# A decoder layer with a gathered and a dense expert mixer on one core: the gather's steps and pace rewritten, four expert blocks' gates kept in SBUF

## The chip, the cores and the metric

One core of a Trainium2 chip runs the whole layer as one program. The metric is the device time of one execution in microseconds; lower is better. The core has a matrix engine (PE), a vector engine (DVE), an activation engine (ACT), a general engine (POOL) and a queue engine (SP), each with its own instruction queue worked off in order, and 16 DMA engines that all of them share.

## The reference

One inference step: attention and mLSTM heads, cross attention, and then the part that matters here, a PEER mixer over 16,384 experts. Each token has 8 heads that choose 16 experts each, so 128 experts with a gate `g`:

```python
e = jnp.take_along_axis(cidx, j, axis=-1)          # 8 x 16 expert numbers per token
g = jax.nn.softmax(sc, axis=-1)
a = g * jax.nn.gelu(jnp.einsum('td,thkd->thk', xb, peer_u[e]))
y = jnp.einsum('thk,thkd->td', a, peer_v[e])
```

`peer_u` and `peer_v` are 16,384 rows of 1,024 float32 each (67 MB each). There are 512 prompt tokens in tiles 0 to 3 of 128, and 32 sample tokens (tile 4).

## The kernel before

Tile 0 goes through all sub-layers first (group 0), then tiles 1 to 3 and the sample tokens together (group 1). The mixer is computed in two ways side by side.

**Gathered tokens** (tiles 0, 3 and 4; class `Gather`). 32 tokens by their 128 experts are one part. For its 32 steps an indirect DMA on POOL's queue gathers 128 rows of one table into a [128, 1024] tile (512 KB): `ru` rows of `peer_u`, of which DVE takes the dot product with the token rows `xr` (`u_load`; three `ru` buffers), or `rv` rows of `peer_v` (`v_load`; six buffers), which PE multiplies, two tiles to a group, by a small matrix `Z` that DVE fills with the gated activations (`v_group`: 4 products, 8 PE instructions, `y<-rv,Z`). Tile 0's u side is done while group 1 runs (`hidden`). What is left for `Gather.steps`, a generator in which each `yield` follows one load, are 4 parts of tile 0 (v side only, 128 loads) and 5 parts of tiles 4 and 3 (u and v, 160 loads each): 448 loads. The old generator has two loops: 4 x 32 v loads of tile 0; then, once the part's choice is known (`G.known`), part after part the u loads of one with the v loads of the part before. Its first part there (tile 4) has no part before it, so 32 u loads stand alone, and the last 32 v loads too.

**Dense tokens** (tiles 1 and 2, 256 tokens; class `Dense`). All 128 blocks of 128 experts are computed. `u_block`: 8 float32 products (16 PE instructions, `ph<-xw,ut`) for the first 40 blocks, and for the other 88, issued from inside the loop below, 24 float32r products (`ph<-xT2..`) of a tile `ut` split into two parts by ACT and DVE; then Gelu into `h`. `gates` builds for each token the 128 x 128 matrix of its gates: DVE and ACT write one-hot tiles `O1` and `O2`, PE multiplies them into `pgt`, ACT copies that to `stg`, and SP writes `stg` to a DRAM tensor `Gd`, one DMA for each of 8 groups of 32 tokens. `v_block`: SP loads `Gt` (gates of four blocks, from `Gd`) and `vt` (two blocks of `peer_v`), DVE makes `a = h * Gt`, `a` and `vt` are split, and PE does 12 float32r products of 512 columns into `yd` (`v_products`).

**What orders them.** A compiler pass schedules instructions by program order as priority. The program order is made by two pacers. `te` adds up a nominal time for each PE product emitted (0.42e-3 a column for float32r, 1.7e-3 for float32; products inside a step are not counted) and runs one step of `Gather.steps` for every `te.every` units. `v` does the same with DVE work and runs one of the first 40 `u_block`s per step. `te.every` is `EVERY3` from the choices (`choices[i].rest()`, DVE's top-16 work) on, and `EVERY4` from block `dn.FIRST` = 13 of the v loop on. With `G.strict` a dot product on DVE also waits for the PE product last emitted.

The end of the program in order: choices (DVE top-16, with early u blocks and gathers), gates (with the last of 40 u blocks), 128 v blocks with u blocks 40 to 127 running 27 ahead, and a layer norm of the two dense tiles. The last two blocks are done one dense tile after the other.

Of the kernel before, what the change touches and what calls it, by code (L numbers as in the profile page):

```python
# [10 lines left out]
F32 = mybir.dt.float32  # L11
F32R = mybir.dt.float32r
# [8 lines left out]
D = 1024  # L21
# [172 lines left out]
def program(ctx, tc, I, O, dbg=None):  # L194
    nc = tc.nc
    dbg = dbg or {}
    s, g = nc.scalar, nc.gpsimd
# [52 lines left out]
    v, te = Vector(nc.vector), Tensor(nc.tensor)  # L250
# [9 lines left out]
    DR = ctx.enter_context(tc.tile_pool(name="scratch", bufs=1, space=bass.MemoryType.DRAM))  # L260
# [51 lines left out]
    right = {}  # L312
# [13 lines left out]
    def split(hi, lo, src):  # L326

        s.copy(hi, src)  # L328
        v.behind(v.tensor_sub(lo, src, hi))

    def parts(raw, hi, lo):
        split(hi, lo, raw)
        return hi, lo
# [103 lines left out]
    TD = 128 * len(DT)  # L437
# [1 line left out]
    memVd = DR.tile([128, 2 * D], F32, name="memVd")  # L439
    x0d = DR.tile([544, D], F32, name="x0d")  # L440
    x2d = [DR.tile([128 if i < 4 else NS, D], F32, name=f"x2d{i}") for i in range(5)]
    Gd = DR.tile([TD // 32, 128, 128, 32], F32, name="Gd")
    eT = {i: P1.tile([128, 128 if i < 4 else NS], I32, name=f"eT{i}") for i in range(5) if i not in DT}
    iT = {}
    gT = {i: P1.tile([128, 128 if i < 4 else NS], F32, name=f"gT{i}") for i in range(5)}
# [1050 lines left out]
    class Gather:  # L1496
# [95 lines left out]
        def steps(self):  # L1592


            us, vs, prev = [], [], None

            parts = [(0, 32 * o) for o in range(4)]
            for o, (i, c) in enumerate(parts):
                p = {"o": o, "parts": parts, "e": eT[i][:, c:c + 32], "hT": gT[i][:, c:c + 32]}
                for k in range(32):  # L1600
                    if k % 2 == 0:
                        rows = []
                    self.v_load(p, k, rows)
                    if k % 2:
                        vs.append((self.late, p, k // 2, rows))
                    vs = [(n - 1, *w) for n, *w in vs]
                    if vs and vs[0][0] < 0:
                        self.v_group(*vs.pop(0)[1:])
                    yield
            parts = []  # L1610
            for r in self.rounds:
                parts += [(r, o) for o in range(len(r))]
            ahead = None
            for n, part in enumerate(parts + [None]):
                p, ahead = ahead, None
                if part and not p:
                    r, o = part
                    while r[o][0] not in self.known:
                        yield
                    p = self.begin(r, o)  # L1620
                for k in range(32):
                    if k == 24 and n + 1 < len(parts) and parts[n + 1][0][0][0] in self.known:
                        ahead = self.begin(*parts[n + 1])
                    if p:
                        us.append(self.u_load(p, k))
                        if prev and self.strict:
                            yield
                    if prev:
                        if k % 2 == 0:
                            rows = []  # L1630
                        self.v_load(prev, k, rows)
                        if k % 2:
                            vs.append((self.late, prev, k // 2, rows))
                    if us and (len(us) == self.ub or not p):
                        us.pop(0)()
                    vs = [(n - 1, *w) for n, *w in vs]
                    if vs and vs[0][0] < 0:
                        self.v_group(*vs.pop(0)[1:])
                    yield
                prev = p  # L1640
            for w in vs:
                self.v_group(*w[1:])

# [36 lines left out]

    def gates(X, PX):

        copy = None
        for tg in range(TD // 32):
            stg = X.tile([128, 128, 32], F32, name="stg", tag="stg", bufs=2)
            i, t0 = DT[tg // 4], 32 * (tg % 4)
            for q in range(8):
                t4 = t0 + 4 * q
                O1 = X.tile([128, 4, 128], F32, name="O1", tag="O1", bufs=4)
                v.tensor_tensor(O1, cst["iota"][:, None, :].to_broadcast([128, 4, 128]), iT[i][:, 0, t4:t4 + 4, None].to_broadcast([128, 4, 128]), op=OP.is_equal)  # L1690
                p = PX.tile([128, 512], F32, name="pgt", tag="pgt", bufs=4)
                for k in range(4):
                    O2 = X.tile([128, 128], F32, name="O2", tag="O2", bufs=12)
                    t = slice(t4 + k, t4 + k + 1)
                    if k:
                        v.tensor_scalar(O2, cst["iota"], iT[i][:, 1, t], gT[i][:, t], op0=OP.is_equal, op1=OP.mult)
                    else:

                        s.activation(O2, cst["iota"], AF.Square, bias=iT[i][:, 2, t])
                        s.activation(O2, O2, AF.Relu, bias=gT[i][:, t], scale=iT[i][:, 3, t])  # L1700
                    te.matmul(p[:, 128 * k:128 * k + 128], O2, O1[:, k], start=True, stop=True)
                if copy:
                    copy()

                def copy(tg=tg, q=q, stg=stg, p=p):
                    s.copy(stg[:, :, 4 * q:4 * q + 4], p.rearrange("p (k j) -> p j k", k=4))
                    if q == 7:
                        nc.sync.dma_start(Gd[tg], stg)
        copy()

    class Dense:
# [3 lines left out]
        def __init__(self, X, XF, PH_, xT):  # L1715
# [7 lines left out]
            for o in (0, 4):  # L1723
                t = right["weights"].tile([128, 4, TD], F32, name="xw", tag="wh", bufs=2)
                v.tensor_add(t, self.xhi[:, o:o + 4], self.xlo[:, o:o + 4])
                self.xw += [t[:, k] for k in range(4)]

        def rows(self, X, c):
            if c % 2 == 0:
                self.two = X.tile([128, 2, D], F32, name="vt", tag="vt", bufs=2)  # L1730
                nc.sync.dma_start(self.two.rearrange("p a d -> p (a d)"), I["peer_v"][128 * c:128 * c + 256].rearrange("(p a) d -> p (a d)", a=2))
            return parts(self.two[:, c % 2], *(X.tile([128, D], F32R, name="vt" + x, tag="vt" + x, bufs=2) for x in "hl"))
# [22 lines left out]

        def v_block(self, X, c):
            n = TD // 32
            if c % 4 == 0:
                self.G = X.tile([128, n, 128], F32, name="Gt", tag="Gt", bufs=2)
                nc.sync.dma_start(self.G.rearrange("p g (a t) -> p g a t", a=4), Gd[:, :, c:c + 4].rearrange("g p a t -> p g a t"))  # L1760
            G = self.G[:, :, 32 * (c % 4):32 * (c % 4) + 32]
            vh_, vl = self.rows(X, c)
            a = X.tile([128, TD], F32, name="a", tag="a", bufs=2)
            by = lambda t: t.rearrange("p (g t) -> p g t", t=32)
            v.tensor_tensor(by(a), by(self.h.pop(c)), G, op=OP.mult)
            ah, al = (X.tile([128, TD], F32R, name=x, tag=x, bufs=3) for x in ("ah", "al"))
            split(ah, al, a)
            return c, ah, al, vh_, vl
# [74 lines left out]
    with tc.tile_pool(name="group0", bufs=1) as Gp:  # L1843
        with weights("weights0", 4):
            xT0 = transposed(0, Gp, xt0)
            rows = sample_index(SL)
# [13 lines left out]
    LATER = 200  # L1860
    EVERY = 2.6
    EVERY2 = 2.6
    EVERY3 = 1.0
    EVERY4 = 1.85
    SKIP = 4
    NZ = 2
    W1 = weights("weights1", 2)
# [33 lines left out]
    dn = Dense(XU, XF, PU, xT2)  # L1901
    EU1 = 3.5
    EU2 = 5.8
# [7 lines left out]
    G.strict = True  # L1911
    te.start(G.steps(), EVERY3)
    for i in (4,) + DT + (3,):
# [2 lines left out]
        G.known.add(i)  # L1916
    stackC.close()
    stackN.close()
    v.every = EU2

    with tc.tile_pool(name="psum gates", bufs=1, space=PSUM) as PX:
        gates(stackC.enter_context(tc.tile_pool(name="gates", bufs=1, side="right")), PX)
    v.finish()
    stackC.close()
    with tc.tile_pool(name="dense v", bufs=1, side="right") as X, tc.tile_pool(name="psum dense", bufs=1, space=PSUM) as PD:
        y = PD.tile([128, len(DT), 1024], F32, name="yd")
        for b in range(NK - 2):
            if b == dn.FIRST:
                stackF.close()
                dn.XT = stackT.enter_context(tc.tile_pool(name="dense ut", bufs=1))  # L1930
                te.every = EVERY4
            if b >= dn.FIRST and b + dn.LA < NK:
                dn.u_block(b + dn.LA)
            w = dn.v_block(X, b)
            for j in range(len(DT)):
                dn.v_products(y, j, *w)

        te.finish()
        last = [dn.v_block(X, b) for b in range(NK - 2, NK)]
        for j in range(len(DT)):  # L1940
            for q in range(2):
                for w in last:
                    dn.v_products(y, j, *w, qs=(q,))
            dn.end(X, y, j)
    stackT.close()
    stackU.close()
    stackG.close()
    stackX.close()

# [13 lines left out]
```

## Time and profile before

| | us |
|---|---|
| median of three runs | 2233.27 (2228.27 to 2234.23) |
| the profiled execution, its own time | 2213.07 |
| its span, first to last instruction | 2211.3 |
| PE busy / DVE / ACT / POOL | 1891.7 / 1427.5 / 677.2 / 833.2 |
| bytes moved by DMA | 625.89 MB, mean 283 GB/s |

A busy PE is a union of pipelined instructions whose ends are modelled, so 99% busy is not 99% of peak. The profile lists each product of float32 as two PE instructions. Times of the trace are from the span's start.

### The profile page before, as it was taken

What the parts mean: (1) busy time and instruction counts of PE and PEld (TensorE: products, weight loads), DVE (VectorE), ACT (ScalarE), POOL (GpSimd) and SP (SyncE); (2) the same over time, 40 slices, a digit from 0 to 9 for tenths busy, and PEclk for the clock granted to TensorE, in tenths of its full rate; (3) what the DMA queues carried; (4) which work ended last, traced back from release to release, by engine and by line L of the source; (5) the groups of instructions that cost most, each with busy time, mean ns of one, the idle gap of its engine ahead of it and who ended that gap; (6) DMA issues with size and microseconds to landing.
All of it is one profiled execution on the core that took longest, in us unless ns stands there. A gap on an engine that the chain in (4) does not pass through costs nothing. (4 is left out here: it accounts for less than half of the span.)

```text
span 2211.3 us, 31987 instructions
## 1 busy us (share of the span) xinstructions
PE 1891.7 (86%) x11579; PEld 1453.3 (66%) x11579; DVE 1427.5 (65%) x3650; ACT 677.2 (31%) x1285; POOL 833.2 (38%) x715
## 2 busy tenths in 40 slices
PE   6998989879787697789899864678998899999997
PEld 4876757759756574567555553446786787786786
DVE  5234334769688784277996476757676777775666
ACT  2121222222333222123112322423343344343443
POOL 3010331026544341130455453445565655563200
PEclk9988999989889897889999985878999999999999
DMA  9626686459957777655799997999999999999854
GB/s 311 215 83 161 177 268 218 164 150 342 286 171 250 261 275 284 232 186 131 272 374 376 351 335 256 340 366 344 386 403 348 377 403 404 402 405 354 305 189 165
DMA packets 213711, 625.89 MB, mean 283 GB/s; under 512 B 23298, under 2 KB 88898, under 8 KB 198578
## 3 DMA queue, kind: packets, MB, share of 16 engines
q0 software_dynamic: 94272, 327.45, 41.3%
q1 hardware_dynamic: 107872, 281.00, 36.1%
q10 hardware_dynamic: 11410, 15.41, 2.0%
q8 instruction: 92, 1.51, 0.3%
q14 instruction: 65, 0.53, 0.1%
HBM read 593.10 MB, written 30.66 MB: 282 GB/s over the span
## 5 line engine op out<-in xcount | busy, mean ns | idle before, releaser
L241 DVE SCALAR_TENSOR_TENSOR ru<-ru,xr 128x1024 f32<-128x1024 f32 x288 | 348.7, 1218 | 200.6 <-DMA ru<-in_peer_u,idx 167.1
L1516 POOL DMA_INDIRECT rv<-in_peer_v,eT x288 | 339.5, 1179 | 311.2 <-PE y L245 240.5
L1516 POOL DMA_INDIRECT ru<-in_peer_u,idx x160 | 211.9, 1325 | 319.4 <-DVE ru L241 162.9
L1673 POOL DMA_INDIRECT ru<-in_peer_u,idx x128 | 166.7, 1302 | 165.2 <-DVE ru L241 106.2
L245 PE MATMUL y<-rv,Z 128*32 128x512 f32 x1152 | 173.8, 651 | 61.6 <-DMA rv<-in_peer_v,eT 41.2
L245 PE MATMUL ph<-xT2h,utl 128*128 128x256 f32 x704 | 202.2, 287 | 15.4 <-DVE utl L241 15.3
L245 PE MATMUL ph<-xT2h,uth 128*128 128x256 f32 x704 | 200.7, 285 | 7.7 <-ACT uth L328 7.5
L245 PE MATMUL ph<-xT2l,uth 128*128 128x256 f32 x704 | 202.8, 288 | 0.0
L245 PE MATMUL yd<-vth,ah 128*128 128x512 f32 x512 | 164.0, 399 | 8.8 <-ACT ah L328 6.8
L245 PE MATMUL yd<-vtl,ah 128*128 128x512 f32 x512 | 163.3, 398 | 7.1 <-DVE vtl L241 7.1
L245 PE MATMUL yd<-vth,al 128*128 128x512 f32 x512 | 163.3, 398 | 0.0
L241 DVE TENSOR_TENSOR vtl<-vt,vth 128x1024 fp32r<-128x1024 f32 x128 | 156.3, 1222 | 10.7 <-ACT vth L328 6.1
L328 ACT CAST vth<-vt 128x1024 fp32r<-128x1024 f32 x128 | 134.4, 1051 | 69.6 <-DMA vt<-in_peer_v 31.9
L245 PE MATMUL ph<-xw,ut 128*128 128x256 f32 x640 | 155.4, 390 | 0.0
L245 PEld LDWEIGHTS ph<-xT2h,utl 128*128 128x128 f32 x704 | 134.6, 191 | 26.9 <-DVE utl L241 16.6
L245 PEld LDWEIGHTS ph<-xw,ut 128*128 128x128 f32 x640 | 118.1, 193 | 50.7 <-issue 31.9
L328 ACT CAST uth<-ut 128x1024 fp32r<-128x1024 f32 x88 | 92.6, 1052 | 187.8 <-PE ph L245 146.8
L245 PEld LDWEIGHTS ph<-xT2h,uth 128*128 128x128 f32 x704 | 136.2, 193 | 20.2 <-issue 8.4
L245 PEld LDWEIGHTS ph<-xT2l,uth 128*128 128x128 f32 x704 | 135.6, 193 | 14.8 <-issue 11.4
L245 PE MATMUL pgt<-O,O 128*128 128x128 f32 x512 | 94.1, 331 | 53.7 <-DVE O L241 51.4
L245 PEld LDWEIGHTS pgt<-O,O 128*128 128x128 f32 x512 | 79.1, 225 | 83.4 <-DVE O L241 56.9
L245 PEld LDWEIGHTS yd<-vtl,ah 128*128 128x128 f32 x512 | 96.5, 190 | 39.4 <-DVE vtl L241 10.5
(541 smaller groups left out, 3717.6 us busy)
## 6 DMA issues: line engine op xcount, KB each, us to landing
vt<-in_peer_v SPq DMA_DIRECT2D x64, 1024.0 KB, 9.4
ut<-in_peer_ut SPq DMA_DIRECT2D x44, 1024.0 KB, 12.3
ut<-in_peer_ut SPq DMA_DIRECT2D x40, 512.0 KB, 6.7
Gd<-stg SPq DMA_DIRECT2D x8, 2048.0 KB, 11.0
Gt<-Gd SPq DMA_DIRECT2D x32, 512.0 KB, 11.8
wz<-in_w_z SPq DMA_DIRECT2D x30, 512.0 KB, 4.8
wo<-in_w_out SPq DMA_DIRECT2D x16, 512.0 KB, 11.1
wz<-in_w_mq SPq DMA_DIRECT2D x16, 512.0 KB, 5.9
```

Of the source, the lines that this page charges most:

```text
L241: return lambda out, *a, **k: self.count(f(out, *a, **k), 0.06 + math.prod(out.shape[1:]) / 960)
L245: return self.count(self.e.matmul(out, l, r, **kw), math.prod(r.shape[1:]) * (0.42e-3 if r.dtype == F32R else 1.7e-3))
L328: s.copy(hi, src)
L1516: self.last = g.indirect_dma_start(out=t, out_offset=None, in_=I[table], in_offset=bass.IndirectOffsetOnAxis(ap=idx, axis=0))
L1673: g.indirect_dma_start(out=t, out_offset=None, in_=I["peer_u"], in_offset=bass.IndirectOffsetOnAxis(ap=idx[:, k:k + 1], axis=0))
```

## The change

`steps` becomes one loop: `ready` holds parts whose v side can run, first the four of tile 0; in each round of 32 steps the v loads of the oldest ready part run beside the u loads of the next part, if that one was begun. The next part is begun at step 24 when its choice is known and at most one part is ready. `EVERY3` goes from 1.0 to 1.25, a new `EVERY5` = 1.65 holds in the gates, and `EVERY4` = 1.75 (was 1.85) holds from block 0 of the v loop on. The gates of blocks 0 to 3 are copied by ACT straight from `pgt` into an SBUF tile `Gt`, which lives in a pool of its own opened ahead of the gates; `Gd` and `stg` hold the other 124. The `peer_v` rows of blocks 0 to 3 are loaded into the weight buffers of the u blocks ahead of the last `Gd` write (`early`). `O2` has 9 buffers for 12.

```diff
--- before.py
+++ after.py
-    Gd = DR.tile([TD // 32, 128, 128, 32], F32, name="Gd")
+    Gd = DR.tile([TD // 32, 128, 124, 32], F32, name="Gd")
...
-            us, vs, prev = [], [], None
+            us, vs, ahead, n = [], [], None, 0
 
             parts = [(0, 32 * o) for o in range(4)]
-            for o, (i, c) in enumerate(parts):
-                p = {"o": o, "parts": parts, "e": eT[i][:, c:c + 32], "hT": gT[i][:, c:c + 32]}
+            ready = [{"o": o, "parts": parts, "e": eT[i][:, c:c + 32], "hT": gT[i][:, c:c + 32]} for o, (i, c) in enumerate(parts)]
+            parts = [(r, o) for r in self.rounds for o in range(len(r))]
+            known = lambda: n < len(parts) and parts[n][0][parts[n][1]][0] in self.known
+            while ready or n < len(parts):
+                p, ahead = ahead, None
+                prev = ready.pop(0) if ready else None
+                if not p and not ready and n < len(parts):
+                    while not known() and not prev:
+                        yield
+                    if known():
+                        p = self.begin(*parts[n])
+                n += p is not None
                 for k in range(32):
-                    if k % 2 == 0:
-                        rows = []
-                    self.v_load(p, k, rows)
-                    if k % 2:
-                        vs.append((self.late, p, k // 2, rows))
-                    vs = [(n - 1, *w) for n, *w in vs]
-                    if vs and vs[0][0] < 0:
-                        self.v_group(*vs.pop(0)[1:])
-                    yield
-            parts = []
-            for r in self.rounds:
-                parts += [(r, o) for o in range(len(r))]
-            ahead = None
-            for n, part in enumerate(parts + [None]):
-                p, ahead = ahead, None
-                if part and not p:
-                    r, o = part
-                    while r[o][0] not in self.known:
-                        yield
-                    p = self.begin(r, o)
-                for k in range(32):
-                    if k == 24 and n + 1 < len(parts) and parts[n + 1][0][0][0] in self.known:
-                        ahead = self.begin(*parts[n + 1])
+                    if k == 24 and known() and len(ready) + (p is not None) <= 1:
+                        ahead = self.begin(*parts[n])
                     if p:
                         us.append(self.u_load(p, k))
                         if prev and self.strict:
...
-                prev = p
+                if p:
+                    ready.append(p)
...
+        G0 = dn.gates_tile()
         for tg in range(TD // 32):
-            stg = X.tile([128, 128, 32], F32, name="stg", tag="stg", bufs=2)
+            stg = X.tile([128, 124, 32], F32, name="stg", tag="stg", bufs=2)
...
-                    O2 = X.tile([128, 128], F32, name="O2", tag="O2", bufs=12)
+                    O2 = X.tile([128, 128], F32, name="O2", tag="O2", bufs=9)
...
-                    s.copy(stg[:, :, 4 * q:4 * q + 4], p.rearrange("p (k j) -> p j k", k=4))
+                    pj = p.rearrange("p (k j) -> p j k", k=4)
+                    s.copy(stg[:, :, 4 * q:4 * q + 4], pj[:, 4:])
+                    s.copy(G0[:, tg].rearrange("p (a t) -> p a t", a=4)[:, :, 4 * q:4 * q + 4], pj[:, :4])
                     if q == 7:
+                        if tg == TD // 32 - 1:
+                            dn.early()
                         nc.sync.dma_start(Gd[tg], stg)
...
+        def gates_tile(self):
+            self.G = self.XW.tile([128, TD // 32, 128], F32, name="Gt", tag="Gt", bufs=2)
+            return self.G
+
+        def early(self):
+
+            self.rows0 = []
+            for c in range(4):
+                t = right["weights"].tile([128, D], F32, name="vt0", tag=("w", "wl")[c % 2], bufs=2)
+                nc.sync.dma_start(t, I["peer_v"][256 * (c // 2):256 * (c // 2) + 256].rearrange("(p a) d -> p a d", a=2)[:, c % 2])
+                self.rows0.append(t)
+
         def rows(self, X, c):
+            if c < 4:
+                return parts(self.rows0[c], *(X.tile([128, D], F32R, name="vt" + x, tag="vt" + x, bufs=2) for x in "hl"))
...
-            if c % 4 == 0:
-                self.G = X.tile([128, n, 128], F32, name="Gt", tag="Gt", bufs=2)
-                nc.sync.dma_start(self.G.rearrange("p g (a t) -> p g a t", a=4), Gd[:, :, c:c + 4].rearrange("g p a t -> p g a t"))
+            if c and c % 4 == 0:
+                nc.sync.dma_start(self.gates_tile().rearrange("p g (a t) -> p g a t", a=4), Gd[:, :, c - 4:c].rearrange("g p a t -> p g a t"))
...
-    EVERY3 = 1.0
-    EVERY4 = 1.85
+    EVERY3 = 1.25
+    EVERY4 = 1.75
+    EVERY5 = 1.65
...
-    v.every = EU2
-
+    v.every, te.every = EU2, EVERY5
+
+    stackW = ExitStack()
+    dn.XW = stackW.enter_context(tc.tile_pool(name="block gates", bufs=1, side="right"))
...
+        te.every = EVERY4
         for b in range(NK - 2):
             if b == dn.FIRST:
                 stackF.close()
                 dn.XT = stackT.enter_context(tc.tile_pool(name="dense ut", bufs=1))
-                te.every = EVERY4
```

## Rows read from the trace of the kernel before

**Rows 1.** The page: the span, and the busy tenths of PE, DVE and DMA and the GB/s in 40 slices of 55.3 us.

```profile
span 2211.3 us, 31987 instructions
...
PE   6998989879787697789899864678998899999997
...
DVE  5234334769688784277996476757676777775666
...
DMA  9626686459957777655799997999999999999854
GB/s 311 215 83 161 177 268 218 164 150 342 286 171 250 261 275 284 232 186 131 272 374 376 351 335 256 340 366 344 386 403 348 377 403 404 402 405 354 305 189 165
```

**Rows 2.** Busy time by stretch, all instructions: choices, gates in three parts, the change-over, blocks 0 to 12, blocks 13 to 92, u and v without gathers, v alone, layer norm. Columns: stretch, its length, busy us of PE, PEld, DVE, ACT and POOL with counts, granted clock, DMA share, GB/s.

```profile
core 0: us, PE busy (x) PEld busy (x) DVE busy (x) ACT busy (x) POOL busy (x), PEclk, DMA share, GB/s
1058.00:1197.00 139.00, 128.62 (x663) 76.02 (x661) 111.47 (x564) 22.83 (x48) 72.82 (x71) 0.98 0.93 348
1197.00:1262.00 65.00, 56.08 (x364) 37.43 (x361) 38.18 (x113) 29.53 (x68) 31.82 (x32) 0.95 0.95 357
1262.00:1366.00 104.00, 63.00 (x299) 49.26 (x302) 73.00 (x154) 28.67 (x65) 51.17 (x46) 0.75 0.86 302
1366.00:1424.00 58.00, 41.78 (x242) 29.57 (x238) 44.79 (x122) 30.57 (x67) 25.23 (x23) 0.84 0.87 319
1424.00:1454.00 30.00, 10.83 (x51) 1.69 (x52) 6.00 (x15) 3.72 (x6) 12.13 (x13) 0.59 1.01 381
1454.00:1520.00 66.00, 49.61 (x194) 33.83 (x194) 44.73 (x73) 19.74 (x26) 29.18 (x23) 0.86 0.98 361
1520.00:2068.00 548.00, 522.92 (x3317) 416.12 (x3317) 378.68 (x609) 216.65 (x319) 303.42 (x224) 0.97 1.00 382
2068.00:2120.00 52.00, 52.00 (x340) 45.14 (x339) 34.15 (x48) 23.55 (x35) 1.95 (x2) 1.00 0.62 220
2120.00:2196.00 76.00, 74.80 (x333) 61.42 (x331) 52.73 (x75) 37.99 (x52) 0.00 (x0) 1.00 0.61 208
2196.00:2211.00 15.00, 3.30 (x14) 2.17 (x12) 10.89 (x20) 0.00 (x0) 1.98 (x2) 0.77 0.19 70
```

**Rows 3.** The gates, 1197 to 1424 us: groups of instructions by line. Columns: count, busy us, mean ns of one, idle time before them and what ended it.

```profile
L245 PE MATMUL pgt<-O,O 128*128 128x128 f32 x512 | 94.1, 331 | 53.7 <-DVE O L241 51.4 <-ACT O L1700 1.2 <-DVE Z L241 0.2
...
L241 DVE TENSOR_SCALAR O<-cst,iT,gT 128x128 f32<-128x128 f32 x189 | 57.9, 351 | 8.2 <-PE pgt L245 7.9
L241 DVE SCALAR_TENSOR_TENSOR ru<-ru,xr 128x1024 f32<-128x1024 f32 x46 | 56.1, 1222 | 39.9 <-DMA ru<-in_peer_u,idx 35.7 <-PE pgt L245 3.2 <-PE ph L245 0.6
L1516 POOL DMA_INDIRECT ru<-in_peer_u,idx x46 | 53.3, 1158 | 61.5 <-DVE O L241 37.8 <-DVE ru L241 17.4 <-DVE hT L241 2.4
L1516 POOL DMA_INDIRECT rv<-in_peer_v,eT x50 | 53.3, 1065 | 52.2 <-PE y L245 43.4 <-PE pgt L245 4.3 <-issue 4.0
...
L241 DVE TENSOR_TENSOR O<-cst,iT 128x512 f32<-128x512 f32 x62 | 42.3, 682 | 0.0
L1706 ACT COPY stg<-pgt 128x512 f32<-128x512 f32 x63 | 36.7, 582 | 91.7 <-PE pgt L245 91.5
```

**Rows 4.** DMA in the same stretch, 1197 to 1424 us: all packets, and POOL's queue of gathers (q0).

```profile
DMA packets 17659, 73.13 MB, mean 322 GB/s; under 512 B 2396, under 2 KB 2396, under 8 KB 16748
...
q0 software_dynamic: 14380, 50.93, 64.0%
```

**Rows 5.** The timeline from the last copy of the gates on, with the first `yd` products of blocks 0 (1453.69), 4 (1467.59), 13 (1517.89) and 101 (2123.58), found by counting 12 `yd` products a block. Columns: start, duration, engine, line, what, and idle time before it.

```profile
1424.02 0.58 ACT L1706 COPY stg<-pgt 128x512 f32<-128x512 f32 x1 [1.92 <-PE pgt L245]
...
1424.63 0.32 SPq L1708 DMA_DIRECT2D Gd<-stg  x1
...
1434.46 0.37 SPq L1760 DMA_DIRECT2D Gt<-Gd  x1
1434.89 2.27 SPq L1731 DMA_DIRECT2D vt<-in_peer_v  x2
...
1444.19 0.76 DVE L241 TENSOR_TENSOR a<-h,Gt 128x256 f32<-128x256 f32 x2 [2.23 <-DMA Gt<-Gd]
...
1447.78 1.99 ACT L328 CAST vth<-vt 128x1024 fp32r<-128x1024 f32 x2 [1.16 <-DMA vt<-in_peer_v]
...
1453.69 1.22 PE L245 MATMUL yd<-vth,ah 128*128 128x512 f32 x2
...
1467.59 0.62 PE L245 MATMUL yd<-vth,ah 128*128 128x512 f32 x2
...
1517.89 1.22 PE L245 MATMUL yd<-vth,ah 128*128 128x512 f32 x2 [0.42 <-ACT ah L328]
...
2123.58 0.61 PE L245 MATMUL yd<-vth,ah 128*128 128x512 f32 x2
```

**Rows 6.** Unit costs, each the busy time of one tile's instructions in one stretch (PE first): `yd` with v blocks alone, `ph` where u and v blocks run without gathers, `y` in blocks 13 to 92.

```profile
2120.00:2190.00 70.00, 69.14 (x306) 57.39 (x307) 0.00 (x0) 1.00 0.62 211
...
2077.00:2120.00 43.00, 23.10 (x185) 23.10 (x186) 2.63 (x7) 1.00 0.53 187
...
1520.00:2068.00 548.00, 68.06 (x488) 9.74 (x488) 8.89 (x13) 0.97 1.00 382
```

**Rows 7.** DMA from 1520 to 2068 us, blocks 13 to 92: all packets, and the GB/s in 40 slices of that stretch.

```profile
GB/s 297 338 352 382 398 410 400 407 404 403 407 395 294 295 277 414 396 412 398 413 397 411 399 409 400 409 396 408 402 407 400 407 404 400 409 343 347 322 400 330
DMA packets 64923, 209.53 MB, mean 382 GB/s; under 512 B 5931, under 2 KB 26635, under 8 KB 54671
```

**Rows 8.** The same stretch, groups by line: DVE's dot products of gathered rows.

```profile
L241 DVE SCALAR_TENSOR_TENSOR ru<-ru,xr 128x1024 f32<-128x1024 f32 x97 | 118.4, 1221 | 124.2 <-DMA ru<-in_peer_u,idx 102.4 <-PE yd L245 10.3 <-PE ph L245 9.1
```

More of the change, by code (lines that the diff above doesn't have):

```diff
@@ L1635, in steps @@
                         us.pop(0)()
-                    vs = [(n - 1, *w) for n, *w in vs]
+                    vs = [(w[0] - 1, *w[1:]) for w in vs]
                     if vs and vs[0][0] < 0:
@@ L1946, in program @@
     stackU.close()
+    stackW.close()
     stackG.close()
```

## The prediction, made before the kernel was run

> **What bounds it now.** Read the 40 slices first [rows 1]: from about 1060 us on DMA stands at 9 tenths nearly throughout, and only the last three slices fall back, to 305, 189 and 165 GB/s. The dip of PE to 6 tenths is in the middle of that. So the gathers use DMA early, and the last 130 us use half of it. The stretches [rows 2] say what each stage is held by. In the choices PE (128.6 of 139 us) and DVE (111.5) are both nearly full. The gates take 227 us, with DVE busy 38.2 + 73.0 + 44.8 = 156 us, PE 161 us and DMA moving 322 GB/s on the mean: nothing is full. The middle part is the worst, 104 us at a granted clock of 0.75: the products wait 51.4 us for `O` on DVE, and DVE itself waits 35.7 us for gathered `ru` rows [rows 3]. That is the stretch where u loads stand alone on three buffers, each dot product blocking DVE's queue, and with it the next `O`. Then come 29.7 us from the last copy at 1424.0 to the first `yd` at 1453.7 [rows 5]: `Gd` must land before `Gt` is issued (1434.5), `vt` stands behind `Gt` on SP, and its cast starts at 1447.8. Blocks 0 to 12 run at 361 GB/s with PE at 50 of 66 us. Blocks 13 to 92 are the long stretch: 548 us, DMA share 1.00 at 382 GB/s and PE busy 522.9. There both are at their limit. After 2068 no gather is left; PE is full and DMA at 0.6.
>
> **The pace in loads.** From the code's nominal units. A float32 u block is 8 x 256 x 1.7e-3 = 3.48 units. Choices: 28 u blocks and some transposes, 99 units, 99 loads before and 99 / 1.25 = 79 after. Gates: 256 products of 128 columns (55.7) and 12 u blocks (41.8), 97.5 units: 97 loads before, and the trace has 46 + 50 = 96 [rows 3], so the count holds; after, 97.5 / 1.65 = 59. Blocks 0 to 12: 12 x 512 x 0.42e-3 = 2.58 units each, 33 loads before, 33.5 / 1.75 = 19 after. From block 13 on u and v are 5.16 units together: 2.79 loads a block before, which uses up the last 220 by block 92; after, 2.95 a block, 260 by block 100, and 31 remain at 1.47 a block, to block 122. A load is 50.93 MB / 96 = 0.53 MB [rows 4]. So 58 loads (31 MB) leave choices and gates, 14 leave blocks 0 to 12, and 71 go behind block 13, 31 of them into the stretch that DMA now half uses.
>
> **Unit costs.** 69.14 / 306 = 0.226 us for a `yd` product, so 2.71 us a v block; 23.10 / 185 = 0.125 for `ph`, 3.0 us a u block; 68.06 / 488 x 8 = 1.12 us for a gather group, which is two v loads [rows 6]. By tile sizes a u and v block moves 0.52 + 0.52 + 0.13 = 1.18 MB, a v block alone 0.66.
>
> **Choices.** 20 loads fewer are 10 groups, at most 11 us of PE. DVE's top-16 work stays. Between 0 and -11: I take -4, since DVE is almost as full as PE.
>
> **Gates.** Three bounds. By bytes: 73.1 MB [rows 4] less 37 loads (19.6), less one layer norm that moves behind (1.5), plus the early `peer_v` rows (2.1): 54 MB, which is 141 us at the 382 GB/s of blocks 13 to 92 and 168 us at this stretch's own 322. By DVE: 64 `O` of 0.682 and 192 of 57.9 / 189 = 0.306 are 102 us, 21 dots of 1.30 are 27, the rest 7: 136 us, and at the old busy share (156 / 227) 198 us. So 141 to 198. In detail: the first 30%, v loads alone, was 65 us at 357 GB/s and PE 56; with 0.6 of the loads, 55 to 60. The rest had 162 us for 98 us of DVE work as it will be; its last part, u and v mixed, kept DVE busy 44.8 / 58 = 77%, so 98 to 127. That makes 153 to 187; I take 171, so -56. What the change adds here is covered: 64 more small ACT copies (below the 0.58 us of the `stg` copy, so under 37 us) on an ACT that was busy 89 of 227; `O2` with 9 buffers still holds two rounds of four.
>
> **Change-over and blocks 0 to 12.** Blocks 0 to 3 need neither `Gd` nor `vt` any more. Block 4 does: `Gt` and `vt` wait on SP behind the last `Gd` write as before, so its cast comes 24 us after the last copy and its first product about 27, where now it comes at 1467.6, 43.6 after [rows 5]. The gain is thus 17 us, not the 30 that the gap shows: what is late next is `Gt` of block 4. If the new tiles must wait until `stg` has been written out (10 us, 1424.6 to 1434.5), blocks 0 to 3 still fit ahead of block 4. Blocks 4 to 12 took 50 us, to 1517.9; now 9 x (0.66 + 1.47 x 0.53) = 13 MB at 382 is 34 us. Sum 62 us for 94, -32, between -16 (no gain in blocks 4 to 12) and -40.
>
> **Blocks 13 to 100.** Before 2123.6 - 1517.9 = 606 us [rows 5]. After: 1.18 + 2.95 x 0.53 = 2.74 MB a block, PE 5.71 + 0.74 x 1.12 = 6.54 us. At 382 GB/s 7.17 us, at the 400 to 410 of the flat part of [rows 7] 6.8. I take 7.05, nearer the mean, since PE is not the limit then: 620 us, +15. Ends: 6.8, -6, and 7.6 at the 361 GB/s of blocks 0 to 12, +62.
>
> **Blocks 101 to 127.** 27 blocks took 76 us [rows 2]; plus 15.5 groups of 1.12: 93; by bytes 22 x 1.44 / 382 = 83 + 14 = 97. I take 96, +20 (17 to 25). The last layer norm of gathered rows falls here, beside a DVE that is busy 52.7 of 76 us.
>
> **Sum.** -4 - 56 - 32 + 15 + 20 = -57. The profiled execution took 2213.07 for a span of 2211.3; 2156 after. The runs' median is 2233.27 / 2213.07 = 1.0091 of it: 2176 us.
>
> **A rule against it.** Blocks 13 to 92 moved 382 GB/s for 548 us, and slices of 400 to 410 follow one another [rows 7]. The Trainium skill, page "DMA: Bandwidth & Descriptors", section "Bandwidth", has about 358 GB/s as what the memory gives one core, and says that this side binds transfers between memory and SBUF. The trace does not agree, by 7% on the mean. An estimate by that page: 2.74 / 358 = 7.65 us a block, 673 us for 88, and the sum would be about nothing.
>
> **Rivals.**
> 1. Gates little shorter: DVE's in-order queue keeps its old busy share, 198 us. For it: `O` waits behind dots whatever the pace. Against it: the u loads no longer stand alone. Then -30: 2203.
> 2. DMA full at its best: gates 141, blocks 13 to 100 at 400 GB/s (602 us, -4), change-over -37, choices -4, the end +17. That is -114: 2118. For it: 200 us at 400 GB/s and more [rows 1]; against it: PE at 6.54 us leaves 4% for every wait.
> 3. The moved bytes pay in full: with more gathers for each block, DMA falls to the 361 GB/s of blocks 0 to 12, which had 33 gathers beside 13 blocks of 0.66 MB [rows 2]. Blocks 13 to 100 +62, the end +25, the change-over -31, the gates and choices as forecast: -4, 2229, no change. This is also where the page's rule ends. Against it: [rows 7].
> 4. Slower: late dots. 97 dots waited 102.4 us for `ru`, 1.05 each [rows 8], with three buffers, and a load is now asked for 5% sooner while DMA is full. DVE does 378.7 / 78 = 4.86 us a block; with 1.48 dots a block for 1.24 it is 5.16, 454 us for 88, plus 130 dots. At 1.05 each that is 591, under 620; at 2.1 it is 727, +122, the sum +50: 2284. It decides from 1.7 us a dot, 7.7 us a block.
>
> **Chances and range.** Forecast 0.55, rival 1 0.20, rival 2 0.13, rival 3 0.07, rival 4 0.05. The forecast's own range, gates 153 to 187 and blocks 13 to 100 within 20 us, is 2145 to 2207. The range reaches down to rival 2 and up over rival 1 to just short of rival 3: 2118 to 2220. A change under 0.3% (6.7 us) cannot be told here. Faster 0.88 (forecast, rivals 1 and 2), same 0.06 (most of rival 3), slower 0.06 (rival 4 and a rest).
>
> **What would show it.** 59 loads between the first `pgt` and the last `stg` copy, and 153 to 187 us there, with no stretch at a clock of 0.75; the first `yd` under 15 us after the last copy and block 4 near 27, held by `Gt` or `vt`; `rv` loads until a few us before the last `yd`; 370 GB/s and more from block 101 on. Wrong if DVE's idle time for `ru` in the blocks passes 1.7 us a dot, if the gates stay above 200 us, or if DMA at share 1.00 shows under 370 GB/s.

## The result and the profile after

The changed kernel took 2154.0 us (median of six runs, 2148.6 to 2159.1) against 2230.8 us (2217.6 to 2238.6) for the kernel before, run beside it: a ratio of 0.964, interval 0.961 to 0.967. That is 77 us less; the forecast was 57. One execution of 4866 us, of the last experiment's second kernel, is left out of all that follows. The first lines of the page after, by 40 slices of 53.8 us:

```profile
span 2152.9 us, 32053 instructions
...
PE   6998989878888778688999998879979979999997
...
DVE  5234324497778786437899687767666757777666
...
DMA  9635675728965859756489999999999999999996
GB/s 320 217 88 138 187 242 184 243 82 269 320 227 177 305 161 355 242 207 218 114 280 350 355 383 390 385 338 399 405 329 371 405 342 369 405 405 405 398 370 228
```

Against [rows 1], PE's dip in slices 24 to 27 has gone from 6, 4, 6 and 7 tenths to 9, 8, 8 and 7, and DMA's last slices stand at 405, 398, 370 and 228 where they stood at 354, 305, 189 and 165. The stages of the changed kernel, in the columns of [rows 2]: choices, gates, blocks 0 to 12 with the change-over, blocks 13 to 100, blocks 101 to 127, layer norm.

```profile
1056.00:1200.00 144.00, 133.79 (x679) 88.89 (x676) 131.08 (x701) 30.18 (x63) 57.45 (x56) 0.99 0.81 292
1200.00:1339.00 139.00, 133.06 (x855) 97.50 (x853) 112.33 (x304) 89.56 (x261) 57.54 (x58) 1.00 0.98 379
1339.00:1399.00 60.00, 48.13 (x218) 33.12 (x219) 42.20 (x75) 23.46 (x35) 22.25 (x19) 0.94 1.01 377
1399.00:2035.00 636.00, 585.36 (x3669) 463.45 (x3667) 444.12 (x717) 239.50 (x354) 356.02 (x268) 0.96 1.01 381
2035.00:2142.00 107.00, 98.40 (x464) 62.12 (x460) 69.88 (x122) 36.14 (x51) 37.63 (x33) 0.98 0.89 329
2142.00:2153.00 11.00, 0.25 (x2) 0.00 (x0) 6.86 (x13) 0.00 (x0) 0.99 (x1) 0.69 0.26 95
```

The same two stages of the kernel before, cut at the same marks (the choices from the last `pm` product ahead of them, and blocks 13 to 100):

```profile
1038.00:1197.00 159.00, 146.63 (x745) 90.80 (x744) 131.23 (x706) 29.98 (x63) 72.82 (x71) 0.98 0.86 318
1518.00:2124.00 606.00, 580.92 (x3680) 466.36 (x3681) 415.48 (x661) 242.00 (x357) 305.64 (x227) 0.97 0.97 367
```

Stage by stage, in us, with the gathered loads issued there:

| stage | before | after | change | forecast | loads before, after |
|---|---|---|---|---|---|
| choices | 158.9 | 143.8 | -15 | -4 | 71, 55 |
| gates | 227.5 | 139.7 | -88 | -56 | 96, 58 |
| last copy to block 13 | 93.3 | 60.1 | -33 | -32 | 35, 19 |
| blocks 13 to 100 | 605.7 | 635.8 | +30 | +15 | 218, 258 |
| blocks 101 to 127 | 76.7 | 106.7 | +30 | +20 | 0, 30 |
| sum | | | -76 | -57 | |

**The two spans must not be subtracted.** 2211.3 - 2152.9 is 58, which looks like the forecast to the microsecond. But the choices, the first place that the change touches, begin at 1038 in one profile and at 1056 in the other, after identical work; in a second profile of the changed kernel (below) they begin at 1040 and its span is 2133.6. Counted from the choices on, the change is -76, as the medians have it.

The gates' groups after, in the columns of [rows 3]:

```profile
L245 PE MATMUL pgt<-O,O 128*128 128x128 f32 x511 | 69.3, 282 | 4.3 <-ACT O L1692 2.2 <-DVE O L241 1.4 <-issue 0.6
...
L241 DVE SCALAR_TENSOR_TENSOR ru<-ru,xr 128x1024 f32<-128x1024 f32 x19 | 23.2, 1224 | 10.4 <-PE pgt L245 4.2 <-DMA ru<-in_peer_u,idx 3.9 <-PE ph L245 2.2
```

Before, PE stood 53.7 us ahead of `pgt`, 51.4 of them for `O`; now 4.3. DVE waited 35.7 us for gathered rows, now 3.9. At a granted clock of 1.00 (before, 0.75 in the middle part [rows 2]) a `pgt` product takes 282 ns for 331, which over 512 products is 25 us of PE time. PE is busy 133 of 139 us.

### The profile page after: what moved, and what is told of

Its sections match the earlier page's. It is cut to its first block, busy times and chain, and to the rows that moved or that the text cites. A ratio compares the mean times of both kernels' runs of the same rounds, so it can differ in the third digit from the quotient of the medians.

```text
span 2152.9 us, 32053 instructions
## 1 busy us (share of the span) xinstructions
PE 1878.7 (87%) x11579; PEld 1437.4 (67%) x11579; DVE 1421.5 (66%) x3650; ACT 676.2 (31%) x1349; POOL 836.5 (39%) x715
## 5 line engine op out<-in xcount | busy, mean ns | idle before, releaser
L245 PEld LDWEIGHTS yd<-vth,al 128*128 128x128 f32 x512 | 96.4, 190 | 35.0 <-issue 15.1
L1086 POOL DMA_INDIRECT kvb<-in_pool_lat,ixk x64 | 63.2, 987 | 135.4 <-PE pn L245 120.2
```

The costliest lines, as they stand in the source:

```text
L245: return self.count(self.e.matmul(out, l, r, **kw), math.prod(r.shape[1:]) * (0.42e-3 if r.dtype == F32R else 1.7e-3))
L1086: g.indirect_dma_start(out=t.rearrange("p a b -> p (a b)"), out_offset=None, in_=I["pool_lat"], in_offset=bass.IndirectOffsetOnAxis(ap=ixk ...
```

## The experiments

Each ratio is to the kernel before, run in the same group on the same chip. There are three groups; the changed kernel was measured again in the second, at 0.9644, and the others are read against that and the 0.964 above.

### The old paces in the new loop

```diff
-    EVERY3 = 1.25
-    EVERY4 = 1.75
-    EVERY5 = 1.65
+    EVERY3 = 1.0
+    EVERY4 = 1.85
+    EVERY5 = 1.0
...
-        te.every = EVERY4
         for b in range(NK - 2):
             if b == dn.FIRST:
...
+                te.every = EVERY4
```

> The new loop and the kept gates with the old paces (1.0 up to block 12, then 1.85): by the pacer's units 99 loads in the choices, 76 in the gates (58 in the changed kernel), 34 in blocks 0 to 12, the last in block 98. Theory (the pace empties the gates' DMA): 66 MB in the gates at 381 GB/s are 173 us, so the gates take 165 to 185 us for the 139.7 of the changed kernel, and blocks 0 to 12 lose 10 to 15; the blocks behind get 12 loads fewer and no gather after block 98, so half comes back: ratio to before 0.96 to 0.975. Rival (the loop: u loads no longer stand alone): the gates stay at 140 to 150 us whatever the pace, ratio 0.945 to 0.955.

2190.5 us, ratio 0.987 (0.979 to 0.995). Choices 157.0, gates 191.9 with 79 loads, block 13 75.2 us after the last copy, blocks 13 to 100 637.0, the end 76.7. The gates and the long stretch:

```profile
1197.00:1388.00 191.00, 146.25 (x863) 109.48 (x865) 142.58 (x365) 90.29 (x263) 91.20 (x82) 0.87 0.93 338
1464.00:2101.00 637.00, 590.13 (x3720) 466.62 (x3720) 428.31 (x686) 241.57 (x356) 324.83 (x246) 0.97 0.98 369
```

With the loop and the kept gates alone the gates lose 36 us; the pace takes 52 more. Over the whole kernel the paces are worth 2.3%. Both theories had the gates too short (165 to 185, and 140 to 150 us) and the ratio too low. The 36 us are not the order of the loads alone, since the loop also leaves 79 loads there for 96. And the u loads, which no longer stand alone, are no less late: dots waited 31.9 us for rows, 0.86 each (35.7 before, 0.78 each [rows 3]), and PE 36.0 us for `O`.

```profile
L245 PE MATMUL pgt<-O,O 128*128 128x128 f32 x511 | 79.6, 306 | 41.2 <-DVE O L241 36.0 <-ACT O L1692 2.5 <-DVE Z L241 1.6
...
L241 DVE SCALAR_TENSOR_TENSOR ru<-ru,xr 128x1024 f32<-128x1024 f32 x37 | 45.2, 1222 | 42.6 <-DMA ru<-in_peer_u,idx 31.9 <-PE pgt L245 7.1 <-PE ph L245 3.5
```

### The old loop at the new paces

```diff
+            for o, (i, c) in enumerate(parts):
...
+            for n, part in enumerate(parts + [None]):
...
-            while ready or n < len(parts):
```

> The old two loops of steps under the new paces, kept gates as in the changed kernel: 79 loads in the choices, 57 in the gates of which 8 are u, 24 u loads alone in blocks 0 to 12 and a little behind. Theory (pace): gates 135 to 150 us as in the changed kernel, blocks 0 to 15 slower by 5 to 15 us because dots of u loads standing alone hold DVE: ratio 0.966 to 0.975. Rival (loop): the gates fall back towards 190 us and the ratio to 0.985 or more.

2164.5 us, 0.977 (0.971 to 0.983). Gates and the stretch to block 13:

```profile
1177.00:1330.00 153.00, 144.65 (x916) 103.40 (x912) 106.36 (x298) 88.91 (x262) 59.37 (x61) 0.96 0.95 360
1330.00:1404.00 74.00, 50.76 (x184) 37.82 (x184) 51.56 (x85) 24.03 (x33) 25.51 (x21) 0.82 0.89 322
```

At the new paces the loop is worth 13 us in the gates, not 36, and 14 after them: the two edits overlap. With nearly as many loads in the gates (59 for 58), 54 of them are v loads for 40, and PE is busy 145 us for 133. The pace theory was nearly met (135 to 150 us, 0.966 to 0.975), the rival's 190 us were not. The u loads that stand alone had moved out of the gates (6 dots there, before 46) into blocks 0 to 12: 21 dots there and not one `rv` load, at a clock of 0.82. Some 10 us come back in blocks 13 to 100 (626 us). Over the whole kernel the loop is worth 1.2%.

### No kept gates, no early rows

```diff
-        G0 = dn.gates_tile()
...
-                        if tg == TD // 32 - 1:
-                            dn.early()
...
-            if c and c % 4 == 0:
+            if c % 4 == 0:
```

> The changed kernel with the gates and the rows of blocks 0 to 3 through DRAM as before. Theory: the first product of block 0 comes 28 to 30 us after the last gate copy for 13.2, block 4 at 40 to 44 for 25.2; 17 us are lost there, and a part comes back since the gathers in flight run on: ratio 0.967 to 0.973. Rival (all behind the gates is set by bytes, and DMA does not stop in the gap): under 5 us lost, ratio below 0.966.

2151.3 us, 0.971 (0.964 to 0.977). The first `yd` comes 26.9 us after the last copy instead of 13.2, block 4 41.7 us after it instead of 25.2, as the theory had it, and block 13 72.3 us instead of 60.1. Of these 12 us some 5 to 9 are left at the end of the program (1102.2 us from the choices on, 1097.2 and 1093.6 in the two profiles of the changed kernel). The ratio's interval overlaps the changed kernel's: a gain of 0 to 14 us, not settled.

### More loads early

```diff
-    EVERY3 = 1.25
-    EVERY4 = 1.75
+    EVERY3 = 1.0
+    EVERY4 = 1.8
```

> The changed kernel with 1.0 in the choices (99 loads for 79) and 1.8 for 1.75 in the blocks (2.87 loads a block for 2.95), 1.65 in the gates. Theory (from block 13 on each load costs its bytes, 0.53 MB at 381 GB/s = 1.4 us, while the choices are full of DVE work and not of bytes: 296 GB/s): choices 139 to 144 us as they are, 7 loads fewer from block 13 to 100 and 13 elsewhere behind the choices; 10 to 25 us faster than the changed kernel, ratio 0.953 to 0.960. Rival (the blocks are bound by waits of DVE and PE, not by bytes): within 5 us of the changed kernel, 0.962 to 0.966.

2140.3 us, 0.965 (0.959 to 0.971): the same as the changed kernel. Choices and gates:

```profile
1044.00:1200.00 156.00, 143.84 (x747) 90.20 (x744) 131.65 (x708) 30.11 (x63) 71.37 (x72) 1.00 0.87 325
1200.00:1330.00 130.00, 123.17 (x807) 97.30 (x810) 116.11 (x311) 89.57 (x263) 51.91 (x48) 0.99 0.95 362
```

16 loads more in the choices cost 12 us, ten fewer in the gates give 10, eight fewer in blocks 13 to 100 give 10, and the change-over and the end lose 7. The theory's gain did not come: a load in the choices isn't free, though DMA has room there (share 0.87). DVE is busy 131 us there with 55 loads and with 71; it is PE's busy time that grows, from 134 to 144 us. The rival's number came true, but not for its reason: blocks 13 to 100 did get shorter.

### The changed kernel once more

> The changed kernel once more, beside the others of this group on one chip: 2148 to 2160 us, so that kernels whose difference is under 1% can be told apart directly and not over the kernel before, whose runs spread over 1.2%.

2135.5 us beside 2214.7 for the kernel before: 0.9644 (0.958 to 0.971). That is under the 2148 to 2160 expected, as this chip is 0.7 to 0.9% quicker for both; the ratio stands. Its stages lie within 2.5 us of the first profile's.

### A visible stop taken away

After 1431.9 PE stands still for 13.7 us, the longest gap in blocks 13 to 100. DVE is waiting there:

```profile
1441.80 1.41 DVE L241 SCALAR_TENSOR_TENSOR xa<-xa,bnr,rv 128x512 f32<-128x512 f32 x2 [13.28 <-DMA rv<-in_lns]
```

The layer norm's constant rows are asked for only when they are needed (the second issue is at 1415.2), and DVE can go on at 1441.8. Asked for two groups sooner:

```diff
-            lnb = [self.X.tile([128, D], F32, name="rv", tag="rv", bufs=self.vb) for _ in range(2)]
-            for k, t in zip((6, 7), lnb):
-                nc.sync.dma_start(t, ...)
+            lnb = self.lnb
...
+            if k == 13 and p["o"] == len(p["parts"]) - 1:
+                self.lnb = [X.tile([128, D], F32, name="rv", tag="rv", bufs=self.vb) for _ in range(2)]
+                ...
```

> The changed kernel, with the two rows of the layer norm for gathered tiles asked for two groups earlier (k = 13 for 15), into rv buffers as before. In the changed kernel DVE waits 13.3 us for them in block 18, with vtl behind it and PE idle for 13.7 us, in a stretch where PE is the fullest engine. Theory A (that stop is paid in full, since PE sets the blocks): 8 to 16 us faster than the changed kernel over the places where it happens. Theory B (bytes set the blocks: the loads in flight go on in the gap and are made up for later): within 4 us.

2147.6 us, 0.969 (0.964 to 0.975): nothing won, and 12 us more than the changed kernel on the same chip (2135.5), which neither theory has; the single executions overlap (2140.6 to 2153.6, and 2133.1 to 2149.1). The wait is gone, but blocks 13 to 100 take 638.7 us. PE stands still elsewhere instead:

```profile
1428.71 1.94 PE L245 MATMUL y<-rv,Z 128*32 128x512 f32 x8 [12.41 <-DMA rv<-in_peer_v,eT]
```

The stop that was removed came back as another. Whether bytes or buffers are the reason this run does not show: the layer norm's rows lie in two of the six `rv` buffers from 1369 and 1381 us until DVE has used them, at 1412 to 1413, and three `rv` loads are issued only then, at 1412.1, 1413.4 and 1414.6.

With the early loads of the run before added:

```diff
-    EVERY3 = 1.25
-    EVERY4 = 1.75
+    EVERY3 = 1.0
+    EVERY4 = 1.8
...
+            lnb = self.lnb
```

> The layer norm's rows earlier and the pace of the run before (1.0 in the choices, 1.65 in the gates, 1.8 in the blocks). The paces alone gave 2140 us. Theory A: another 8 to 16 us on that, 2124 to 2134. Theory B: 2136 to 2142.

2151.4 us, 0.969 (0.964 to 0.975), above both forecasts. Blocks 13 to 100 take 623 us (626 with the paces alone), the change-over to block 13 69 (64). No version tried that does the same work beats the changed kernel.

### Half the dense rows

```diff
-                nc.sync.dma_start(self.two..., I["peer_v"][128 * c:128 * c + 256]...)
+                nc.sync.dma_start(self.two[:, 0], I["peer_v"][128 * c:128 * c + 128])
...
-                    nc.sync.dma_start(self.ut, I["peer_ut"][b // 2])
+                    nc.sync.dma_start(self.ut[:, :D], I["peer_ut"][b // 2][:, :D])
```

> The changed kernel, in which the dense blocks load only half of their u and v rows and use that half twice (its y for the two dense tiles is therefore another; every instruction on PE, DVE, ACT and POOL is as it was): 0.52 MB a block less, 2.2 for 2.74 MB. Theory B (bytes set blocks 13 to 100): 636 us fall to PE's floor, 585 to 600, and the wait of a dot for its rows from 1.14 us to under 0.5. Theory A (PE with DVE's in-order stops): 615 or more, and the dots wait nearly as long.

2081.7 us (one run). Blocks 13 to 100, and the dots in them:

```profile
1384.00:1970.00 586.00, 570.38 (x3666) 457.16 (x3665) 453.02 (x718) 243.97 (x356) 334.52 (x268) 0.99 0.97 337
```

```profile
L241 DVE SCALAR_TENSOR_TENSOR ru<-ru,xr 128x1024 f32<-128x1024 f32 x130 | 158.7, 1221 | 44.3 <-DMA ru<-in_peer_u,idx 21.9 <-PE yd L245 18.5 <-PE ph L245 3.3
```

The answering line of the changed kernel, 1399 to 2035 us:

```profile
L241 DVE SCALAR_TENSOR_TENSOR ru<-ru,xr 128x1024 f32<-128x1024 f32 x129 | 157.8, 1224 | 146.5 <-DMA ru<-in_peer_u,idx 119.7 <-PE ph L245 11.7 <-PE yd L245 10.4
```

With the same instructions and 45 MB less, the stretch falls from 636 to 586 us, the dots wait 0.34 us each for 1.14, and PE is busy 570 us: theory B in all three. The packets are as many (76,293 for 75,711), so it is the bytes in them that count. So bytes do set the long stretch, and PE's own floor is only 8 to 10% below it. The share of DMA stays at 0.97, though, at 337 GB/s and with PE busy 97% of the time. A share near 1 alone does not show that DMA is the limit; the GB/s and PE's column must be read with it.

### The gates without gathers

```diff
-    EVERY5 = 1.65
+    EVERY5 = 1e9
...
-        te.every = EVERY4
+        te.every, te.held = EVERY4, 0.0
```

> The changed kernel with no gather step run in the gates; the 59 loads go behind, 54 of them as one heap after block 125. What the gates cost without gathers: PE has 512 instructions of pgt and 12 u blocks, about 100 us with the products, DVE 64 x 0.68 + 192 x 0.31 = 102 us. If the changed kernel's gates (137 to 140 us in three profiles) are held by the gathers' bytes and products, they fall to 105 to 118 us here, so that a load costs 0.4 to 0.6 us in the gates for 1.3 in the blocks; if DVE's and PE's hand-over of one-hot tiles holds them, they stay above 128. The whole kernel is slower than the changed one by 40 us or more, since the heap at the end runs alone.

2184.0 us (one run; 2217.8 before). The gates:

```profile
1184.00:1286.00 102.00, 102.00 (x716) 92.15 (x718) 85.16 (x247) 85.52 (x262) 2.15 (x2) 1.00 0.61 229
```

PE is never idle: 102 us is its floor here, just under the 105 to 118 forecast. Two loads are left in the stage, so the 56 more of the changed kernel cost 36 to 38 us, 0.65 each; the step from 58 to 79 in the run at the old paces costs 52, 2.5 each (it has 37 u loads for 18, and a clock of 0.87). The loads come back at the end: 42 run behind the last block, with a tail of 90 us instead of 11, and the whole kernel is some 45 us slower than the changed one, as expected.

### More buffers for the dots

Dots wait for `ru` whatever the pace, so buffers of the other table were given to `ru`, in the kernel before (five and four) and in the changed one (four and five).

```diff
-... 3, 6, 3)
+... 5, 4, 3)
```

> The kernel before with five ru and four rv buffers for three and six (the same memory); nothing else. If its gates are long because u loads stand alone on three buffers and their dots hold DVE, the wait of a dot there falls from 0.87 us to under 0.5 and the gates from 227 to 195 to 212 us. If it is the number of loads in the gates (96, 73 MB), they stay within 8 us of 227. Later stretches may lose by the rv buffers.

```diff
-... 3, 6, 3)
+... 4, 5, 3)
```

> The changed kernel with four ru and five rv buffers for three and six. If waits of dots (1.14 us each in blocks 13 to 100) cost time by themselves, blocks 13 to 100 fall by 10 to 25 us from 636 and the kernel is 0.5 to 1.2% faster than the changed one, ratio 0.952 to 0.959; if those waits are only where bytes make themselves felt, it stays within 8 us, ratio 0.961 to 0.969.

2281.5 us, 1.030 (1.025 to 1.035), and 2170.5 us, 0.981 (0.976 to 0.986), more than either theory had for the second. In the blocks the dots' idle time falls from 1.28 to 0.20 us each in the first, and from 1.14 to 0.57 in the second, and both are slower than the kernels that they come from. In the gates of the first the dots' waits for rows fall from 35.7 to 11.6 us, and the gates stay at 226 us for 227 (86 loads for 96), as the rival had it. DVE is busy 66% of them (69% before), and PE now waits 28.5 us for `rv` rows (9.8 before):

```profile
1243.00:1469.00 226.00, 161.06 (x901) 117.38 (x899) 149.04 (x375) 89.11 (x202) 94.30 (x90) 0.85 0.85 298
```

```profile
L241 DVE SCALAR_TENSOR_TENSOR ru<-ru,xr 128x1024 f32<-128x1024 f32 x39 | 47.0, 1223 | 28.1 <-PE pgt L245 15.3 <-DMA ru<-in_peer_u,idx 11.6 <-PE ph L245 0.4
```

The dots and PE's waits of the first, 1555 to 2192 us (637 us for the same blocks), and its choices (195 us for 159, PE waiting 28.6 us for `rv` rows where it waited 3.0):

```profile
L241 DVE SCALAR_TENSOR_TENSOR ru<-ru,xr 128x1024 f32<-128x1024 f32 x104 | 127.0, 1221 | 20.4 <-PE yd L245 17.1 <-PE ph L245 2.7
```

```profile
PE y L245 <- DMA rv<-in_peer_v,eT: 27.6, 13, 5.3
```

```profile
1048.00:1243.00 195.00, 155.03 (x739) 97.38 (x738) 132.17 (x706) 30.04 (x64) 70.74 (x73) 0.93 0.77 267
```

DVE's wait has become PE's. As each edit changes two counts, what a `ru` buffer alone would do was not measured.

## Why the prediction was right, and where its terms were off

**Counts of loads: right but for the choices.** 16 loads leave the choices (71 to 55), not 20. 59 forecast in the gates, 58 issued; 19 in blocks 0 to 12, 19; 260 in blocks 13 to 100, 258; 31 left, 30.

**Gates: right in direction, mis-sized by 32 us, and the cause that was named is not shown.** Forecast 171 us between 141 and 198, measured 139.7. The step that failed is the detailed one, which kept the old speed in each part: 55 to 60 us for the first, a DVE busy share of 77% for the rest. With 58 loads for 96, 19 of them dots for 46, the share went up to 81% (112 of 139 us).

The prediction laid the old share to u loads that stand alone, whose late rows hold DVE and so `O`. Two runs speak against that as the whole cause. In the new loop at the old paces u loads do not stand alone and their rows are as late, in gates of 192 us. With five `ru` buffers dots waited 0.30 us for rows in place of 0.78 (11.6 / 39, 35.7 / 46), in gates as long as before, though two `rv` buffers were given up for it. What goes with shorter gates in all runs with three and six buffers is fewer loads in them: 102, 130 to 132, 136 to 141, 192 and 227 us for 2, 48, 58, 79 and 96 loads, and 153 us for the 59 of the old loop, most of them v loads.

The measured time lies at the low bound, 54 MB at 382 GB/s: it is 52.67 MB at 379 GB/s. A bound that the forecast did not list lies close below: PE, 133 of 139 us. No run tells which of the two holds the stage.

**Choices: outside their own bounds.** Forecast -4 in 0 to -11, measured -15. The stretch read began at 1058 [rows 2], 20 us after the choices do, and the bound priced a group at 1.12 us of PE. Here the `y` products take 10.5 us less for 8 groups, 1.3 each, and PE is busy 13 us less (146.6 to 133.8), while DVE's 131 us stay. With the buffers unchanged the choices took 155.7 to 158.9 us in the kernels at 1.0 and 143.2 to 145.2 in those at 1.25: 10 to 16 us for 16 loads, or 0.7 to 1 us a load.

**Change-over and blocks 0 to 12: right in number, in part for another reason.** Forecast 62 us, block 0 under 15, block 4 near 27; measured 60.1, 13.2 and 25.2. What holds block 0 is the case that the prediction put in an if-sentence:

```profile
1339.26 0.33 SPq L1704 DMA_DIRECT2D Gd<-stg  x1
...
1346.68 0.37 SPq L1769 DMA_DIRECT2D Gt<-Gd  x1
1346.80 1.05 ACT L328 CAST vth<-vt 128x1024 fp32r<-128x1024 f32 x1 [7.49 <-DMA Gd<-stg]
1346.90 0.76 DVE L241 TENSOR_TENSOR a<-h,Gt 128x256 f32<-128x256 f32 x2 [4.23 <-DMA Gd<-stg]
```

The new tiles wait until `stg` is written out. `Gt` or `vt` was to hold block 4; instead its products follow block 3's without a gap. In the kernel without kept gates the same places are later:

```profile
1330.99 0.37 SPq L1750 DMA_DIRECT2D Gt<-Gd  x1
...
1350.17 1.22 PE L245 MATMUL yd<-vth,ah 128*128 128x512 f32 x2 [5.95 <-ACT vth L328]
```

**Blocks 13 to 100: +30, forecast +15.** The rate taken lay between the mean of 382 and the plateau of 400 to 410. The mean held, over 242.00 MB:

```profile
GB/s 400 326 301 369 380 401 410 398 411 401 401 350 305 305 332 361 412 401 406 407 400 341 302 337 332 392 401 413 398 410 403 399 413 399 408 404 401 410 399 383
DMA packets 75711, 242.00 MB, mean 381 GB/s; under 512 B 7334, under 2 KB 30486, under 8 KB 64653
```

The plateaus are as high as before, and the dips to 300 are there as before. The dips lie where a part of gathered tokens begins: its token rows `xr` (512 KB) are asked for at 1418.2, 1581.3 and 1749.3 us, in slices 2, 12 and 23 of these 40, and before at 1523.4 and 1691.1. What lowers the rate there was not tested. A mean has dips in it and had to be taken whole: 2.74 MB at 382 is 7.17 us a block, the step's own first value; 7.22 was measured. The Trainium skill, page "DMA: Bandwidth & Descriptors", section "Bandwidth", has about 358 GB/s as the limit of one core for transfers between memory and SBUF; further up, the same section has it as what each of two streaming cores gets. The 381 GB/s over 636 us again do not agree with it as the limit of this core; what the neighbouring core did is not on record. The forecast built on that limit (no change) fell.

**Blocks 101 to 127: +30, forecast +20.** To the last load at 2111.8 they move 380 GB/s at share 1.00, as the blocks before. The last 30 us, with the gathered layer norm in them, have PE busy only 25; the forecast had no idle time there. Two of its signs failed here: the last load is issued 30 us ahead of the last `yd`, not a few us, and the mean of the whole stretch is 329 GB/s, not 370.

**The rivals.** The gates at 198 us fell. DMA at its best was right for the gates (141) and wrong for the blocks, where the 400 GB/s did not last. The fall to 361 GB/s did not come. Late rows cost 0.93 us a dot (119.7 / 129; 1.05 before), far from 1.7; with every idle time before a dot it is 1.14 for 1.28.

**The balance.** The terms that were too cautious (choices and gates, 43 us) outweigh those that were too low (the blocks, 25), which leaves -76 for -57. That the total came as near as this is in part luck, since the errors have opposite signs. The forecast's own range, 2145 to 2207, is narrower than its two ends added up (2137 to 2212); 2154 lies in both. And 1.0091 as the ratio of median to profile did not carry over, since the changed kernel's profiled run of 2154.7 us is at its median.

**Open.** At the old paces blocks 13 to 100 took 637 us too, with 238 loads for 258 and 369 GB/s. That mean is of 616 us with gathers, at 375 GB/s, and of 21 us behind the last load, at 199 GB/s, in which PE is never idle. At 381 the first part would have been some 10 us shorter; those bytes alone don't explain.

## What to carry to other kernels

Moving a load pays by the difference between its prices in the two stages: here 2.5 us in the gates above 58 loads and 0.65 below, with the mix of u and v loads that these runs had, and about 0.9 in the blocks (60 us for 70 loads more). Take loads out of a stage until its own engine is full; moving more won nothing here (with more loads early the gates gave 10 us and the choices took 12). And compare profiles from the first stage that the change touches, not by their spans.

## What the runs showed of the chip that was not expected

Identical work ahead of the choices ended between 1034 and 1056 us in different executions, a spread larger than several of the terms forecast. Buffers that cut the dots' idle time by 84% (1.28 to 0.20 us a dot) left a kernel 3% slower, since they came from `rv` and PE then waited for those rows. And 16 DMA engines showed a share of 0.97 at 337 GB/s and of 1.01 at 381, with as many packets.
